# Gate and up projections by Strassen's seven products, operands in two hand-managed SBUF arenas

## The chip, the core and the metric

The kernel runs on one core of a Trainium2 chip, as one launch. The metric is the device time of an execution in microseconds; the medians compared here are of several executions. A profiled execution gives the trace from which all rows below are taken; its span is the time from its first to its last recorded work.

## What is computed

One decoder block over 512 tokens of width 2048, all in float32. Two token mixers run in parallel (latent attention with 16 heads, and a gMLP-style spatial gating unit), their outputs are merged by sigmoid gates, projected and added to the input, and a SwiGLU feed-forward of width 5632 and a last RMSNorm follow:

```
a = rms_norm(h, norm_mix_g);  z = a @ w_in            # q_lat, kv_lat, k_pe, uv, gate_logits
y_attn = mla(q_lat, kv_lat, k_pe, ...) @ w_o_attn;    y_sgu = sgu(uv, ...) @ w_o_sgu
merged = gates[0] * y_attn + gates[1] * y_sgu
h = h + merged @ w_out
f = rms_norm(h, norm_ffn_g)
h = h + (silu(f @ w_gate_ffn) * (f @ w_up_ffn)) @ w_down_ffn      # w_gate, w_up: 2048 x 5632
return rms_norm(h, norm_final_g)
```

## The kernel before

Every large product is made with float32 operands that are split into a high part (`fp32r`, rounded by a ScalarE cast) and a low part (source minus high, one VectorE subtraction). A product is then three matmuls into one PSUM bank: low x high, high x high, high x low (`mm3`, lines 98 to 101). A matmul takes 128 x 128 weights and up to 512 moving columns.

Weights lie in DRAM in blocks of 512 KB (128 partitions x 1024 floats). `chunk` (line 89) loads one block by SP's queue into a `raw` tile of the pool `wraw` (4 buffers), casts it on ScalarE (line 94) and subtracts on VectorE (line 95) into `whi` and `wlo` (3 buffers each). `gemm_fm` uses a block as the stationary operand (features come out on partitions, 512 tokens in the free dimension): 8 products, so 24 matmuls. `gemm_tm` uses it as the moving operand (tokens come out on partitions), 24 matmuls as well. Everything else is a 128 x 512 tile of one pool `big` (75 buffers), handed out by `T()`.

The stages follow each other in the text: latents, rotary tables, spatial gating unit, attention by pairs of heads, attention output, gates and merge, output projection with residual, feed-forward. Intermediate results stay in SBUF. In the feed-forward, `norm_in` transposes each quarter of `h` (line 546) and splits it into `fT` as soon as that quarter of `h` is there; the factor 1/rms of the tokens is applied after the matmuls, by a row `rfb` that is multiplied onto the PSUM banks (lines 582 and 584). `hidden(mp)` makes 256 of the 5632 hidden features: four blocks of w_gate and four of w_up alternate, 192 matmuls of 512 columns; there are 22 of them, 4224 matmuls. After 6 or 8 tiles of hidden features `down` multiplies them with their rows of w_down and adds into `h`. The last block of `down` and the final norm run by token blocks.

The order on each engine is set by a scheduler that arranges the written instructions by its own estimates; on the chip each engine then works through its list in that order, and semaphores make it wait for its operands.

Of the kernel before, what the change touches and what calls it, by code (L numbers as in the profile page):

```python
# [9 lines left out]
F32 = mybir.dt.float32  # L10
# [31 lines left out]
BIG, WR, WS = 75, 4, 3  # L42
FMAX = float(np.finfo(np.float32).max)


@with_exitstack
def tile_block(ctx: ExitStack, tc, a):
# [9 lines left out]
    def T(dt=F32):  # L57
        return big.tile([P, 512], dt, tag="t", name="t")
# [4 lines left out]
    def small(n, tag):  # L63
        return sml.tile([P, n], F32, tag="s%d" % n, name=tag)

# [8 lines left out]
    ones = con[:, C_ONE:C_ONE + P]  # L74

    def split(src, gain=None, n=512):
        hi, lo = T(F32R), T(F32R)
        if n < 512:
            hi, lo, src = hi[:, :n], lo[:, :n], src[:, :n]
        if gain is None:  # L80
            nc.scalar.copy(hi, src)  # L81
            nc.vector.tensor_tensor(out=lo, in0=src, in1=hi.bitcast(F32), op=ALU.subtract)  # L82
        else:
            nc.scalar.activation(hi, src, AF.Copy, scale=gain)
            nc.vector.scalar_tensor_tensor(
                out=lo, in0=src, scalar=gain, in1=hi.bitcast(F32), op0=ALU.mult, op1=ALU.subtract)
        return hi, lo

    def chunk(src, n=1024):
        raw = wraw.tile([P, 1024], F32, tag="raw", name="raw")  # L90
        hi = wsp.tile([P, 1024], F32R, tag="whi", name="whi")
        lo = wsp.tile([P, 1024], F32R, tag="wlo", name="wlo")
# [3 lines left out]
        return hi[:, :n], lo[:, :n]  # L96
# [6 lines left out]
    def gemm_fm(banks, w, kq, xs, first, last):  # L103
        """banks[m] += w[k-quad, 256 columns]^T @ xs (feature-major)."""
        hi, lo = chunk(w)
        hi = hi.rearrange("p (k m) -> p k m", k=4)
        lo = lo.rearrange("p (k m) -> p k m", k=4)
        for m, ps in enumerate(banks):
            ms = slice(m * P, (m + 1) * P)
            for k in range(4):  # L110
                xh, xl = xs[kq * 4 + k]
                mm3(ps, hi[:, k, ms], lo[:, k, ms], xh, xl, first and k == 0, last and k == 3)

    def gemm_tm(banks, w, kp, xs, first, last):
        """banks[tb] += xs^T @ w[k-pair, 512 columns] (token-major)."""
        hi, lo = chunk(w)
        for tb, ps in enumerate(banks):
            ts = slice(tb * P, (tb + 1) * P)
            for k in range(2):
                xh, xl = xs[kp * 2 + k]  # L120
                ws = slice(k * 512, (k + 1) * 512)
                mm3(ps, xh[:, ts], xl[:, ts], hi[:, ws], lo[:, ws], first and k == 0, last and k == 1)

    def rsqrt(ss, width, n, tag):
        """1/sqrt(ss/width + eps) with one Newton step behind the table's square root."""
# [13 lines left out]
    def sumsq(parts, n, tag):  # L139
        """Sum of squares along the free axis of each list of tiles: [P, n]."""  # L140
        k = len(parts[0])
        acc = small(n * k, tag + "a")
        for i, tiles in enumerate(parts):
            for j, t in enumerate(tiles):
                junk = T()
# [7 lines left out]
    def row_bcast(r, tag):  # L153
        """[P, NB] per-token columns -> the same values along the free axis on each partition."""
        ps = PS()
        for tb in range(NB):
            dg = T()[:, :P]
            nc.vector.tensor_scalar(out=dg, in0=ident, scalar1=r[:, tb:tb + 1], scalar2=None, op0=ALU.mult)
            nc.tensor.matmul(ps[:, tb * P:(tb + 1) * P], ones, dg, start=True, stop=True)  # L159
        out = T()  # L160
# [4 lines left out]
    def load_x(xs, k):  # L165
        """Tiles 2k and 2k + 1 of the gained x, feature-major."""
        raw = wraw.tile([P, 1024], F32, tag="raw", name="raw")
        nc.sync.dma_start(raw, a["xT"][k])
        for j in range(2):
            v = V_MIX + k * 2 + j  # L170
            xs.append(split(raw[:, j * 512:(j + 1) * 512], vec[:, v:v + 1]))

# [3 lines left out]
    def x_stats(tb):  # L176
        for c in range(4):
            t, junk = T(), T()
            nc.sync.dma_start(t, a["x"][tb * P:(tb + 1) * P, c * 512:(c + 1) * 512])
            nc.scalar.activation(junk, t, AF.Square, accum_out=xacc[:, tb * 4 + c:tb * 4 + c + 1])  # L180

# [34 lines left out]
    posi = big.tile([P, 512], I32, tag="t", name="posi")  # L216
# [11 lines left out]
    sinT = cst.tile([P, 512], F32, name="sinT")  # L228
    cosT = cst.tile([P, 512], F32, name="cosT")
# [3 lines left out]
    nc.scalar.activation(cosT, ang, AF.Sin)  # L233

    def rope(src):
        """The rotated [2 x 64 rope features, tokens]."""
        rot, out = T(), T()
# [4 lines left out]
        nc.vector.tensor_tensor(out=out, in0=out, in1=rot, op=ALU.add)  # L242
        return out

# [1 line left out]
    raw = wraw.tile([P, 1024], F32, tag="raw", name="raw")  # L246
    nc.sync.dma_start(raw, a["w_kpe"])
    kps = PS()
    for half in range(2):
        wk = wsp.tile([P, 1024], F32R, tag=("whi", "wlo")[half], name="wk").rearrange("p (k o m) -> p k o m", k=8, o=2)  # L250
# [7 lines left out]
    rxb = row_bcast(rx, "rxb")  # L258
    kpe = T()
    for own, other in ((slice(0, 64), slice(64, 128)), (slice(64, 128), slice(0, 64))):  # L260
        nc.scalar.copy(kpe[own], kps[other])
        nc.vector.tensor_tensor(out=kpe[own], in0=kps[own], in1=kpe[own], op=ALU.add)
    nc.vector.tensor_tensor(out=kpe, in0=kpe, in1=rxb, op=ALU.mult)
# [6 lines left out]
    vv = [[None, None] for _ in range(NB)]  # L270
    for g in range(2):
        banks = [PS() for _ in range(NB)]
        for kp in range(8):
            gemm_tm(banks, a["w_v"][g, kp], kp, aT, kp == 0, kp == 7)
        for tb, ps in enumerate(banks):
            t = T()
            nc.scalar.activation(t, ps, AF.Gelu_apprx_tanh, scale=rx[:, tb:tb + 1])
            vv[tb][g] = t
    rv = rsqrt(sumsq(vv, NB, "sv"), SGUW, NB, "rv")
    for tb in range(NB):  # L280
        for g in range(2):
            nc.vector.tensor_scalar(out=vv[tb][g], in0=vv[tb][g], scalar1=rv[:, tb:tb + 1], scalar2=None,
                                    op0=ALU.mult)

    kpe = rope(kpe)
    kph = cst.tile([P, 512], F32R, name="kph")
    kpl = cst.tile([P, 512], F32R, name="kpl")
    nc.scalar.copy(kph, kpe)
    nc.vector.tensor_tensor(out=kpl, in0=kpe, in1=kph.bitcast(F32), op=ALU.subtract)

    ut = []
    for mp in range(4):
        banks = [PS(), PS()]
        for kq in range(4):
            gemm_fm(banks, a["w_u"][mp, kq], kq, aT, kq == 0, kq == 3)
        for ps in banks:
            t = T()
            nc.vector.tensor_tensor(out=t, in0=ps, in1=rxb, op=ALU.mult)
# [430 lines left out]
```

## Time and profile before

| | us |
|---|---|
| median of 3 runs | 2789.36 |
| lowest and highest | 2789.19, 2790.16 |
| profiled execution, span | 2788.1 |
| TensorE busy in it | 2769.5 |
| VectorE, ScalarE busy in it | 1125.1, 843.1 |
| bytes read from HBM | 273.92 MB, 100 GB/s over the span |

The medians lie 1.3 us above the profiled span. Busy times of TensorE are sums of records that overlap: a 512-column matmul is recorded with 0.39 us and its successor starts 0.23 us later, so spacing, not duration, tells what a matmul costs in a stream. The same holds, by some 0.09 us, for records of VectorE that follow each other without a wait. "PEld" is TensorE's weight load, which runs beside the matmuls.

### The profile page before, as it was taken

How to read it: one execution, taken by the hardware profiler on the slowest of the kernel's cores; microseconds unless marked ns; L12 is line 12 of the kernel's file. 1: busy time of each engine (PE TensorE's matmuls, PEld its weight loads, DVE VectorE, ACT ScalarE, POOL GpSimd, SP SyncE). 2: the span in 40 equal slices, each digit the busy share in tenths (PEclk: the TensorE clock that was granted, in tenths of full speed). 3: DMA queues.
4: the chain of work that ended last, by engine and by line, in shares of the span. 5: the costliest groups of instructions: out<-in, count | busy, mean ns of one | idle time of the engine just before them, and what ended most of it. 6: DMA issues, size and time to landing. Idle time of an engine off the chain costs nothing.

```text
span 2788.1 us, 30320 instructions
## 1 busy us (share of the span) xinstructions
PE 2769.5 (99%) x12712; PEld 2312.9 (83%) x12712; DVE 1125.1 (40%) x1470; ACT 843.1 (30%) x1195; POOL 15.4 (1%) x31
## 2 busy tenths in 40 slices
PE   8999999999999999999999999999999999999998
PEld 7888988888888888888888888888888888888887
DVE  3433867742433333532433333333333333343345
ACT  5332565621322222332322122212221222222223
POOL 0000000000000000100000000000000000000000
PEclk9999999999999999999999999999999999999999
DMA  7323211222423322432223323323222322223232
GB/s 249 101 91 96 79 53 54 70 90 97 154 97 98 98 98 93 153 102 91 91 98 98 99 92 98 98 98 99 94 96 98 98 99 96 94 98 98 99 121 91
DMA packets 79752, 280.07 MB, mean 100 GB/s; under 512 B 9152, under 2 KB 9152, under 8 KB 79616
## 3 DMA queue, kind: packets, MB, share of 16 engines
q1 hardware_dynamic: 76176, 268.99, 29.4%
q0 software_dynamic: 2000, 6.56, 0.7%
q10 hardware_dynamic: 1440, 2.60, 0.3%
q8 instruction: 99, 1.62, 0.2%
q14 instruction: 37, 0.30, 0.0%
HBM read 273.92 MB, written 4.19 MB: 100 GB/s over the span
## 4 chain that ended last, share of the span: by engine, by line
PE 99%; DVE 0%; DMA 0%; ACT 0%; issue 0%; SPq 0%
PE b L99 32%; PE b L101 32%; PE b L100 32%; PE b L446 1%; PE b L425 0%; PE b L426 0%; PE b L546 0%; PE b L341 0%; DMA raw<-in_w_lat 0%; PE b L328 0%; ACT whi L94 0%; DVE wlo L95 0%; PE b L159 0%; DVE t L266 0%; DVE t L82 0%
## 5 line engine op out<-in xcount | busy, mean ns | idle before, releaser
L95 DVE TENSOR_TENSOR wlo<-raw,whi 128x1024 fp32r<-128x1024 f32 (+1 forms) x480 | 583.3, 1216 | 1416.0 <-ACT whi L94 1415.7
L99 PE MATMUL b<-t,wlo 128*128 128x512 f32 x2592 | 1008.8, 389 | 0.0
L101 PE MATMUL b<-t,whi 128*128 128x512 f32 x2592 | 1008.5, 389 | 0.0
L100 PE MATMUL b<-t,whi 128*128 128x512 f32 x2592 | 1008.5, 389 | 0.0
L94 ACT CAST whi<-raw 128x1024 fp32r<-128x1024 f32 (+1 forms) x480 | 501.6, 1046 | 1588.7 <-PE b L101 977.2
L99 PEld LDWEIGHTS b<-t,wlo 128*128 128x128 f32 x2592 | 486.6, 188 | 101.5 <-DVE wlo L95 0.2
L101 PEld LDWEIGHTS b<-t,whi 128*128 128x128 f32 x2592 | 486.6, 188 | 100.9
L100 PEld LDWEIGHTS b<-t,whi 128*128 128x128 f32 x2592 | 486.6, 188 | 100.7
L99 PE MATMUL b<-whi,t 128*128 128x512 f32 (+1 forms) x1280 | 486.3, 380 | 7.9 <-ACT whi L94 7.9
L101 PE MATMUL b<-wlo,t 128*128 128x512 f32 (+1 forms) x1280 | 485.5, 379 | 0.0
L100 PE MATMUL b<-whi,t 128*128 128x512 f32 (+1 forms) x1280 | 485.3, 379 | 0.0
L99 PEld LDWEIGHTS b<-whi,t 128*128 128x128 f32 x1280 | 241.4, 189 | 52.7 <-ACT whi L94 7.9
L101 PEld LDWEIGHTS b<-wlo,t 128*128 128x128 f32 x1280 | 241.3, 188 | 45.8 <-DVE wlo L95 0.8
L100 PEld LDWEIGHTS b<-whi,t 128*128 128x128 f32 x1280 | 241.4, 189 | 45.1
L596 DVE TENSOR_TENSOR t<-b,t 128x512 f32<-128x512 f32 x96 | 66.1, 689 | 32.4 <-PE b L101 31.9
L81 ACT CAST t<-t 128x512 fp32r<-128x512 f32 x84 | 49.3, 623 | 98.4 <-DVE t L585 96.4
L82 DVE TENSOR_TENSOR t<-t 128x512 fp32r<-128x512 f32 x84 | 55.7, 689 | 32.9 <-ACT t L81 32.9
L99 PE MATMUL b<-t 128*128 128x512 f32 (+2 forms) x192 | 66.3, 346 | 1.2 <-DVE t L82 1.2
L100 PE MATMUL b<-t 128*128 128x512 f32 (+2 forms) x192 | 66.3, 345 | 0.0
L101 PE MATMUL b<-t 128*128 128x512 f32 (+2 forms) x192 | 66.2, 345 | 0.0
L82 DVE TENSOR_TENSOR t<-b,t 128x512 fp32r<-128x512 f32 (+1 forms) x96 | 58.2, 662 | 15.6 <-ACT t L81 15.3
L81 ACT CAST t<-b 128x512 fp32r<-128x512 f32 (+1 forms) x96 | 49.1, 586 | 30.0 <-PE b L101 29.8
(187 smaller groups left out, 950.3 us busy)
## 6 DMA issues: line engine op xcount, KB each, us to landing
raw<-in_w_gate SPq DMA_DIRECT2D x88, 512.0 KB, 3.3
raw<-in_w_up SPq DMA_DIRECT2D x88, 512.0 KB, 3.3
raw<-in_w_down SPq DMA_DIRECT2D x88, 512.0 KB, 3.3
raw<-in_w_g SPq DMA_DIRECT2D x64, 512.0 KB, 3.3
raw<-in_w_oattn SPq DMA_DIRECT2D x32, 512.0 KB, 3.3
raw<-in_w_out SPq DMA_DIRECT2D x32, 512.0 KB, 3.3
raw<-in_xT SPq DMA_DIRECT2D x16, 512.0 KB, 4.6
raw<-in_w_lat SPq DMA_DIRECT2D x16, 512.0 KB, 4.5
```

The lines of the kernel that those rows point to most:

```text
L81: nc.scalar.copy(hi, src)
L82: nc.vector.tensor_tensor(out=lo, in0=src, in1=hi.bitcast(F32), op=ALU.subtract)
L94: nc.scalar.copy(hi[:, :n], raw[:, :n])
L95: nc.vector.tensor_tensor(out=lo[:, :n], in0=raw[:, :n], in1=hi[:, :n].bitcast(F32), op=ALU.subtract)
L99: nc.tensor.matmul(ps, sl, mh, start=first, stop=False)
L100: nc.tensor.matmul(ps, sh, mh, start=False, stop=False)
L101: nc.tensor.matmul(ps, sh, ml, start=False, stop=last)
L446: nc.tensor.transpose(out=pb[b][:, c:c + P], in_=src, identity=ident)
L596: nc.vector.tensor_tensor(out=h[tb][c], in0=ps, in1=h[tb][c], op=ALU.add)
```

## The change

**Gate and up.** A matrix product of 2 x 2 blocks can be made with seven block products instead of eight (the form used is Winograd's, with 15 sums). `forms_x` makes seven forms of each pair of feature tiles: of the blocks b11 and b12 (even feature tile, first and last 256 tokens) and b21 and b22 (odd tile). A form is a 512-wide tile that holds its high part in the first 256 columns and its low part in the last. `pair_gemm` (44 calls: 22 times w_gate, 22 times w_up) loads the four blocks of 256 output columns into one `raw` tile of 4096 floats per partition, sees them as quarters a11, a21, a12 and a22 that each run through all four blocks, makes the sums s1 to s4 on VectorE (s3, s2 and s4 overwrite a21, a11 and a12), and splits each of the seven operands (`form_w`). `product` issues, for each of 8 steps, one matmul of the high weights against the whole 512-wide form (high and low part side by side) and one of the low weights against the 256 high columns. Three PSUM banks collect the seven products, and VectorE and ScalarE add them up into the output.

**Normalisation.** `h` is multiplied by 1/rms before it is transposed, after all of W_out, and the transposed tiles become forms; no factor is applied after the matmuls.

**Memory.** The pools `big`, `wraw` and `wsp` are replaced by two tiles, `ar` (144 units of 256 floats per partition, high and low parts) and `af` (52 units, float tiles), from which an `Arena` hands out spans when the program is written: `get(n)` looks at starts at multiples of n (16 for 16) and takes the span whose latest release is oldest; spans of under 4 units avoid the first 32 units of `af`. `drop` gives spans back. The 112 units of the forms leave 32 units of `ar` for split weights: four pairs of high and low part.

**Spills.** For that space, gelu outputs (`utd`), the mixed tiles (`sgd`), attention heads (`ogd`), both branches' outputs (`ysd`, `ytd`), `h` (`hd`) and the hidden features (`hidd`) are written to DRAM and read back, mostly by POOL's queue. All hidden features are made before `down` starts; `down` runs over groups of 8 tiles, the next group being loaded and split while one is multiplied.

```diff
+class Arena:
...
+    def get(self, n):
+        best = None
+        for i in range(0, len(self.free_at) - n + 1, n if n < 16 else 16):
+            span = self.free_at[i:i + n]
+            if None not in span:
+                cost = (n < 4 and i < self.keep, max(span), -i)
+                if best is None or cost < best[0]:
+                    best = cost, i
...
+    def put(self, *aps):
+        for ap in aps:
+            _, i, n = self.held.pop(id(ap))
+            self.clock += 1
+            self.free_at[i:i + n] = [self.clock] * n
...
+    ar = Arena(cst.tile([P, NR * 256], F32R, name="ar"), NR)
+    af = Arena(cst.tile([P, NF * 256], F32, name="af"), NF, 32)
...
+        for src in (b11, b21, b22, t4, t1, t2, t3):
+            f = ar.get(2)
+            nc.scalar.copy(f[:, :256], src)
+            nc.vector.tensor_tensor(out=f[:, 256:], in0=src, in1=f[:, :256].bitcast(F32), op=ALU.subtract)
...
+    def form_w(src):
+        hi, lo = ar.get(4), ar.get(4)
+        hv, lv = (t.rearrange("p (k m) -> p k m", m=P) for t in (hi, lo))
+        nc.scalar.copy(hv, src)
+        nc.vector.tensor_tensor(out=lv, in0=src, in1=hv.bitcast(F32), op=ALU.subtract)
+        return hi, lo
+
+    def product(ps, w, i, first):
+
+        hi, lo = w
+        for kp in range(8):
+            ks = slice(kp * P, (kp + 1) * P)
+            x = fx[kp][i]
+            nc.tensor.matmul(ps, hi[:, ks], x, start=first and kp == 0, stop=False, skip_group_check=True)
+            nc.tensor.matmul(ps[:, :256], lo[:, ks], x[:, :256], start=False, stop=kp == 7, skip_group_check=True)
+        drop(w)
...
+    def pair_gemm(w):
+
+        raw = af.get(16)
         for kq in range(4):
-            gemm_fm(bg, a["w_gate"][mp, kq], kq, fT, kq == 0, kq == 3)
-            gemm_fm(bu, a["w_up"][mp, kq], kq, fT, kq == 0, kq == 3)
...
+            nc.sync.dma_start(raw[:, kq * 1024:(kq + 1) * 1024], w[kq])
+        quarters = raw.rearrange("p (k q m) -> p k q m", q=4, m=P)
+        a11, a21, a12, a22 = (quarters[:, :, q, :] for q in range(4))
+        ba, bb, bd = bank(), bank(), bank()
+        out = [T(), T()]
...
+        st = af.get(4)
+        s1 = st.rearrange("p (k m) -> p k m", m=P)
+        product(ba, form_w(a11), 0, True)
+        tt(s1, a21, a22, ALU.add)
+        s3 = tt(a21, a11, a21, ALU.subtract)
+        s2 = tt(a11, s1, a11, ALU.subtract)
+        u, u2, v = T(), T(), T()
+        nc.scalar.copy(u, ba)
+        product(bb, form_w(s2), 5, True)
+        tt(u2, bb, u, ALU.add)
+        product(bd, form_w(s3), 6, True)
+        product(bb, form_w(s1), 4, False)
+        tt(v, bb, u, ALU.add)
+        tt(v, bd, v, ALU.add)
+        both(c22, v)
+        drop(v)
+        product(ba, form_w(a12), 1, False)
+        nc.scalar.copy(c11, ba[:, 256:])
+        tt(c11, ba[:, :256], c11, ALU.add)
+        s4 = tt(a12, a12, s2, ALU.subtract)
+        product(bb, form_w(s4), 2, False)
+        tt(u, bb, u, ALU.add)
+        both(c12, u)
+        product(bd, form_w(a22), 3, False)
+        tt(u2, bd, u2, ALU.add)
+        both(c21, u2)
+        drop(u, u2)
+        drop(raw, st)
+        return out
```

What the scheduler made of it is seen at three places. First SP's queue, in the middle of gate and up; `DVE_49` is VectorE's semaphore, `DMAHW` those of earlier loads. Before:

```order
L93 DMA raw<-in_w_gate 128x1024 [waits DMAHW7_49,DVE_49]
L93 DMA raw<-in_w_up 128x1024 [waits DMAHW0_49,DVE_49]
L93 DMA raw<-in_w_gate 128x1024 [waits DMAHW1_49,DVE_49]
L93 DMA raw<-in_w_up 128x1024 [waits DMAHW2_49,DVE_49]
L93 DMA raw<-in_w_gate 128x1024 [waits DMAHW3_49,DVE_49]
```

and now:

```order
L725 DMA af<-in_w_gate 128x1024 [waits DMAHW7_49,DVE_49]
L725 DMA af<-in_w_gate 128x1024 [waits DMAHW0_49]
L725 DMA af<-in_w_gate 128x1024 [waits DMAHW1_49]
L725 DMA af<-in_w_gate 128x1024 [waits DMAHW2_49]
L725 DMA af<-in_w_up 128x1024 [waits DMAHW3_49,DVE_49]
L725 DMA af<-in_w_up 128x1024 [waits DMAHW4_49]
```

Each block waited for its own buffer before; now four blocks go together behind one wait for VectorE. Second ScalarE, over one pair (L701 is the cast of `form_w`, L738 the copy of `ba` to `u`, L748 that to c11, L764 Silu; `PE_49` and `Activation_49` are the semaphores of TensorE and ScalarE):

```order
L701 CAST ar<-af 128x1024 [waits DMAHW2_49,DMAHW7_49,DMAHW1_49,DMAHW0_49]
L701 CAST ar<-af 128x1024 [waits DVE_49,PE_49,Activation_49]
L764 ACTIVATE af<-af 128x512 [waits DVE_49]
L701 CAST ar<-af 128x1024 [waits DVE_49]
L701 CAST ar<-af 128x1024 [waits PE_49,Activation_49]
L738 COPY af<-b 128x512 [waits PE_49]
L701 CAST ar<-af 128x1024 [waits DVE_49]
L701 CAST ar<-af 128x1024 [waits DVE_49,PE_49,Activation_49]
L701 CAST ar<-af 128x1024 [waits PE_49]
L748 COPY af<-b 128x256 [waits PE_49]
```

Where one cast for each block stood before, seven casts and two copies stand now, and the copy of the first product has two casts that wait for TensorE around it. Third VectorE at the start of a pair (L702 is the low part of `form_w`; L107 are the sums, 128x1024 being s1 and 128x8x128 s3, s2 and s4):

```order
L107 TENSOR_TENSOR af<-af 128x1024 [waits DMAHW5_49,DMAHW6_49,DMAHW4_49,DMAHW3_49]
L107 TENSOR_TENSOR af<-b,af 128x512 [waits PE_49]
L702 TENSOR_TENSOR ar<-af,ar 128x1024 [waits Activation_49]
L107 TENSOR_TENSOR af<-af 128x256 [waits DVE_49]
L107 TENSOR_TENSOR af<-af 128x8x128
L107 TENSOR_TENSOR af<-af 128x512 [waits DVE_49]
L107 TENSOR_TENSOR af<-af 128x8x128 [waits DVE_49]
L702 TENSOR_TENSOR ar<-af,ar 128x1024 [waits Activation_49]
```

The low part of a11 stands third, behind s1 and behind an addition that reads the last bank of the pair before.

## Rows read from the trace of the kernel before

**Rows 1.** Page, part 1: busy us of each engine, share of span, instructions

```profile
PE 2769.5 (99%) x12712; PEld 2312.9 (83%) x12712; DVE 1125.1 (40%) x1470; ACT 843.1 (30%) x1195; POOL 15.4 (1%) x31
```

**Rows 2.** Waits: ScalarE's longest; us in total, times, longest

```profile
ACT whi L94 <- PE b L101: 977.2, 285, 4.7
```

**Rows 3.** Windows: stretch, length, busy (instructions) by engine, clock, DMA share, GB/s

```profile
1440.00:1700.00 260.00, 260.00 (x1148) 215.29 (x1148) 90.26 (x96) 60.21 (x64) 0.00 (x0) 1.00 0.30 96
```

**Rows 4.** Timeline, TensorE, values projection: start us, duration us, what

```profile
334.41 0.28 PE L101 MATMUL b<-wlo,t 128*128 128x256 f32 x1
...
339.80 0.28 PE L101 MATMUL b<-wlo,t 128*128 128x256 f32 x1
```

**Rows 5.** Groups by shape, VectorE: count, busy us, mean ns, idle before

```profile
L95 DVE TENSOR_TENSOR wlo<-raw,whi 128x1024 fp32r<-128x1024 f32 x464 | 568.1, 1225 | 1396.7 <-ACT whi L94 1396.4
L427 DVE CUSTOM_DVE_ANT_0 t<-b,con 128x256 f32<-128x256 f32 x16 | 6.8, 423 | 8.2 <-PE b L426 7.5
L253 DVE TENSOR_TENSOR wk<-raw,wk 128x512 fp32r<-128x512 f32 x2 | 1.3, 688 | 3.8 <-ACT wk L252 3.8
```

**Rows 6.** Timeline, VectorE, operations back to back in the feed-forward

```profile
1386.68 1.22 DVE L95 TENSOR_TENSOR wlo<-raw,whi 128x1024 fp32r<-128x1024 f32 x1
1387.81 0.68 DVE L582 TENSOR_TENSOR t<-b,t 128x512 f32<-128x512 f32 x1
1388.41 0.68 DVE L584 TENSOR_TENSOR t<-b,t 128x512 f32<-128x512 f32 x1
```

**Rows 7.** Groups by shape, ScalarE

```profile
L94 ACT CAST whi<-raw 128x1024 fp32r<-128x1024 f32 x464 | 488.9, 1054 | 1569.4 <-PE b L101 968.0 <-PE b L100 498.3 <-issue 98.4
L81 ACT CAST t<-b 128x512 fp32r<-128x512 f32 x80 | 45.3, 600 | 30.0 <-PE b L101 29.8
```

**Rows 8.** DMA issues: KB each, median us from issue to landing

```profile
raw<-in_w_gate SPq DMA_DIRECT2D x88, 512.0 KB, 3.3
t<-in_x POOLq DMA_DIRECT2D x16, 256.0 KB, 4.4
```

**Rows 9.** Timeline, SP's queue, start of the kernel: four loads of 512 KB

```profile
0.81 0.39 SPq L168 DMA_DIRECT2D raw<-in_xT  x1
...
2.19 0.47 SPq L93 DMA_DIRECT2D raw<-in_w_lat  x1
```

**Rows 10.** Windows at the start of the kernel, columns as in rows 3

```profile
3.00:4.00 1.00, 0.00 (x0) 0.00 (x0) 0.00 (x0) 0.00 (x0) 0.00 (x0) 1.00 1.03 402
8.00:9.00 1.00, 1.00 (x2) 0.42 (x2) 1.00 (x1) 0.61 (x1) 0.00 (x0) 1.00 1.04 426
```

**Rows 11.** Chain in order of time, and DMA issues, first 5 us

```profile
1.25 5.55 DMA raw<-in_w_lat
...
raw<-in_w_lat SPq DMA_DIRECT2D x2, 512.0 KB, 6.5
con<-in_consts ACTq DMA_DIRECT2D x1, 448.5 KB, 6.2
```

**Rows 12.** Timeline, TensorE: transposes of one quarter of `h`

```profile
1203.53 2.04 PE L546 MATMUL b<-con,t 128*128 128x128 f32 x16
```

**Rows 13.** Timeline, VectorE: the small operations of 1/rms, first and last

```profile
100.77 0.16 DVE L127 TENSOR_SCALAR rlv<-lacc 128x8 f32<-128x8 f32 x1
...
102.05 0.17 DVE L136 TENSOR_TENSOR rlo<-rlr,rlt 128x8 f32<-128x8 f32 x1
```

**Rows 14.** Timeline, TensorE, its first matmuls

```profile
7.92 0.80 PE L99 MATMUL b<-whi,t 128*128 128x512 f32 x1 [7.92 <-ACT whi L94]
...
13.56 0.40 PE L99 MATMUL b<-whi,t 128*128 128x512 f32 x1
```

**Rows 15.** Timeline, TensorE, after a wait late in attention

```profile
557.60 0.50 PE L99 MATMUL b<-t 128*128 128x512 f32 x1 [1.22 <-DVE t L82]
...
558.18 0.40 PE L101 MATMUL b<-t 128*128 128x512 f32 x1
```

**Rows 16.** Groups, TensorE's weight loads

```profile
L100 PEld LDWEIGHTS b<-whi,t 128*128 128x128 f32 x1280 | 241.4, 189 | 45.1
```

More of the change, by code (lines that the diff above doesn't have):

```diff
@@ L171, in load_x @@
             xs.append(split(raw[:, j * 512:(j + 1) * 512], vec[:, v:v + 1]))
+        drop(raw)
     aT = []
@@ L242, in rope @@
         nc.vector.tensor_tensor(out=out, in0=out, in1=rot, op=ALU.add)
+        drop(rot)
         return out
-    raw = wraw.tile([P, 1024], F32, tag="raw", name="raw")
+    raw = af.get(4)
     nc.sync.dma_start(raw, a["w_kpe"])
@@ new lines, in tile_block @@
+    qnT, kvT = latT
+    rv = rsqrt(sumsq(vv, NB, "sv"), SGUW, NB, "rv")
+    for tb in range(NB):
+        for g in range(2):
+            nc.vector.tensor_scalar(out=vv[tb][g], in0=vv[tb][g], scalar1=rv[:, tb:tb + 1], scalar2=None,
+                                    op0=ALU.mult)
+    rope(kp0, kpe)
+    kph = ar.get(2)
+    kpl = ar.get(2)
+    nc.scalar.copy(kph, kpe)
+    nc.vector.tensor_tensor(out=kpl, in0=kpe, in1=kph.bitcast(F32), op=ALU.subtract)
+    drop(kp0, kpe)
+    utd = drm.tile([G, P, 512], F32, name="utd")
@@ L377, in q_rope @@
             out.append(t)
+        drop(pe)
         return out
@@ L435, in scores @@
             out.append(dst)
-        return out
+        drop(qs, qp, ks)
+        return out, tiles
     def transposed(pr):
@@ L455, in values, with load @@
             mm3(ps[:, q0:], vh[:, o:o + P], vl[:, o:o + P], ph, pl, j == 0, j == NB - 1)
+        return ps
+    ogd = drm.tile([KD, P, 512], F32, name="ogd")
+    ytd = drm.tile([KD, P, 512], F32, name="ytd")
+    ysd = drm.tile([KD, P, 512], F32, name="ysd")
+    def load(src):
         t = T()
-        nc.vector.tensor_copy(t, ps)
+        nc.gpsimd.dma_start(t, src)
         return t
@@ L493, in tile_block, with gate @@
         for kq in range(4):
-            if mp == 0 and kq >= 2:
-                oT[kq * 4:kq * 4 + 4] = [split(t) for t in oT[kq * 4:kq * 4 + 4]]
             gemm_fm(banks, a["w_oattn"][mp, kq], kq, oT, kq == 0, kq == 3)
-        for ps in banks:
+            if mp == 7:
+                drop(oT[kq * 4:kq * 4 + 4])
+        for i, ps in enumerate(banks):
             t = T()
             nc.vector.tensor_copy(t, ps)
-            mrg.append(t)
+            nc.gpsimd.dma_start(ytd[mp * 2 + i], t)
+            drop(t)
     aT = []
-    def gate(w, b, mp, load=False):
+    mrg = []
+    def gate(w, b, mp, load=False, last=False):
         banks = [PS(), PS()]
@@ new lines, in tile_block, with hidden @@
+    for mp in range(DFF // 256):
+        gate = pair_gemm(a["w_gate"][mp])
+        for t in gate:
+            nc.scalar.activation(t, t, AF.Silu)
+        for i, t in enumerate(pair_gemm(a["w_up"][mp])):
+            tt(t, t, gate[i], ALU.mult)
+            nc.gpsimd.dma_start(hidd[mp * 2 + i], t)
+            drop(t, gate[i])
+    drop(fx)
+    for tb in range(NB):
+        for c in range(4):
+            h[tb][c] = load(hd[tb, :, c * 512:(c + 1) * 512])
+    def hidden(k0, n):
+        return [move(load(hidd[k])) for k in range(k0, k0 + n)]
```

382 lines of the change are left out of this document (217 added, 165 removed).

## Prediction, made before the run

> **What bounds the kernel now.** I read the busy totals first: TensorE is busy for 2769.5 of the 2788.1 us span [rows 1]. The waits come next: ScalarE's casts, on which VectorE's subtractions follow, stand idle for TensorE for 977 us [rows 2], so before the change any work on these two is free until it makes TensorE wait. TensorE's rate comes last. In a stretch of pure 512-column matmuls, 260 us hold 1148 of them, 0.2265 us each [rows 3]; that is the number to use, not the 0.39 us of one record, since records overlap. For 256 columns the values projection shows 45 steps between 334.41 and 339.80, 0.120 us each [rows 4].
>
> **The gain on TensorE.** Gate and up took 4224 matmuls of 512 columns: 4224 x 0.2265 = 957 us. Now each of the 44 calls of `pair_gemm` (a "pair" below: one weight matrix, 256 output columns) issues 7 products of 8 steps, a 512 and a 256 each: 56 x (0.2265 + 0.120) = 19.4 us, 854 us for all 44. Alternating widths are not in the trace; the two pure rows bound them. If TensorE never waited, 103 us would be gone.
> [...]
>
> **VectorE and ScalarE as engines.** Per pair VectorE has 11 operations of 1024 elements, 5 or 6 of 512 and 4 of 256. Records last 1.225, 0.688 and about 0.42 us [rows 5], but back to back a 1024 takes 1.13 and a 512 0.60 [rows 6]; I take 0.35 for a 256. Sum 12.4 + 3.3 + 1.4 = 17.1 us, under 19.4. The new operands are strided by quarters; the strided key weights of L253 take 688 ns for 512, like contiguous ones [rows 5], so no surcharge. ScalarE has 7 casts of 1024, two copies and a Silu, some 9 us [rows 7]. Neither is the bound by its sum. The question is the order in which they wait.
>
> **The load is not double-buffered.** `raw` takes 16 units at 0, 16 or 32 of the float arena. 32 nearly always holds some T tile. `st` (4 units) may lie anywhere and lands in 0, the half that was free longest; `drop(raw, st)` then gives `st` the later clock, so half 0 counts as younger than half 16, and the next `raw` takes half 16 again, the one just released. Working the allocator through, 42 of 44 pairs load into the same half. The SP rows show the result: the first of each four loads waits for VectorE, that is for the low part of a22, the last reader of `raw`. ScalarE's first cast then waits for all four landings, because every quarter runs through all four blocks.
> The landing of 2 MB: a lone 512 KB takes 3.3 us [rows 8]. At the start of the kernel four such loads are issued from 0.81 to 2.19 us [rows 9] and the engines move 402 to 426 GB/s [rows 10]. So 3.3 + 3 x 0.524 MB / 0.41 = 7.1 us. From the other side: the two w_lat loads took 5.55 and, with their median at 6.5, 7.45 us, so the last landed at 9.64, 8.8 us after the first issue, with a further 448 KB among them worth 1.1 us [rows 11]: 7.7. I take 7.4, between 6.5 (first bytes earlier) and 8.8.
> [...]
>
> **One pair, step by step**, from the landing as zero, with 0.05 us for a semaphore. ScalarE casts a11 high, 0.05 to 1.10; TensorE's first matmul at 1.15. The second needs a11 low, which stands on VectorE behind s1 (1.14) and an addition of the pair before (0.60): ready at 3.02. TensorE idles 1.7. The first product issues until 5.6. Then the order puts one matmul of a12's product, into the same bank, ahead of s2's; it needs the a12 cast (0.95 to the next) and the copy of the bank to u (0.6): 7.4, TensorE idles 1.8. Then s2's cast: 8.4, idles 0.75. The products of s2 and s3 end at 14.1, which frees the weight slot for a22: cast and low part until 16.5. Four loads: 16.5 + 7.4 = **23.9 us**.
> TensorE's own loop is as long: 19.4 plus the waits. If the load came early, a11's low part would still stand behind the addition that waits for the previous pair's last product: 0.2 + 0.6 + 1.23 against one matmul, a wait of 1.85; 19.4 + 1.85 + 1.8 + 0.75 = 23.8. So a faster load saves next to nothing and a slower one costs in full: 23.5 to 25.3 us. 44 x 23.9 = 1052, against 957: **+95 us** (+77 to +156).
>
> **The rest.**
> - Entry to the gate: the normalisation was applied after the matmuls and its transposes ran inside TensorE's stream, 64 of them, 2.04 us per 16 [rows 12], 8 us in all. Now everything waits for the last W_out column: add, square, statistics (0.69 + 0.82 + 1.28 table + 1.45 for the small VectorE chain [rows 13], some 4 us), then 8 scalings and 88 operations of 256 elements on VectorE (0.40 and 0.33 back to back: 32 us) against 8 scalings, 16 copies and 56 casts of 256 on ScalarE (0.64, 0.60 and, carried on below the two widths of [rows 7], some 0.34: 34 us), which alternate, then the first a11 forms, 3 us. 43 minus 8: **+35** (28 to 45).
> - Into attention: gelu tiles go to DRAM and back; w_sgu's load (256 KB by POOL, as in_x 4.4 us [rows 8]) now waits for the T slots of the last gelu tiles, and the first query weights for slots that the mixing holds: one round trip of 4.4 + 0.6 + transposes and one of slot release + 3.3 + 2.2, some 7 and 15 us: **+22** (5 to 35), since nothing lies beside them on TensorE.
> - Into down: the first w_down blocks wait for float and weight slots that the last pair holds: release + 3.3 + 1.05 + 1.23 behind 16 splits: **+12** (5 to 25). `hidd` is read early and lies beside it.
> - The other spills (ysd, ytd, ogd, the x reload) are POOL loads and stores beside 150 us stretches of matmuls: 0. That cover is W_osgu's 7 groups for the attention output; without it one load and split, 6 us.
> [...]
>
> **Rivals.**
> - *TensorE always finds its operands* (faster): a pair at 19.4 us is -103, with +77 for the rest 2762 us. It decides below (957 - 77) / 44 = 20.0 us a pair, waits under 0.6 us. The SP order and the three chained ScalarE steps speak against it. 2%; another 2% for the space between it and 2900, half of it within the bound of no change.
> - *The load is slower*: the stores of `hidd` or strided reads slow it to 10 us or more. The load loop is then 26.5 us, 44 x 2.6 = +114, some 3075 us. For it: spills share the engines. Against: before, they moved 96 GB/s [rows 3] and now little more. 8%.
> - [...] 5%. [...]
> - *The 256-column matmul is bound by its weight load*, 189 ns a record [rows 16]: +0.068 x 56 = 3.8 us a pair on TensorE's loop, 44 x 3.7 = +163, 3125 us. The 0.120 spacing, each with its own weights, speaks against it. 3%.
>
> **How the numbers follow.** Span 2788.1 + 95 + 35 + 22 + 12 + 8 = 2960; the median stands 1.3 us above the span: **2961 us**. This case has 80%, from 2900 (all low ends but one: 77 + 28 + 5 + 5 = 115) to 3060 (156 + 45 + 35 + 25 + 15 = 276, short of all high ends at once). The rivals lie outside; 2 in 10 are left out. A measurement of this kernel tells 0.2% (5.6 us) from no change. Faster 0.02, within it 0.01, slower 0.97.
>
> **What the next profile would show.** The four loads of a pair issued about 16 us after the landing before, and landing 7 to 8 us later; a cast at L701 waiting for them; TensorE at L712 waiting for VectorE and at L711 for ScalarE, some 1.8 us each, and busy about 81% over 1050 us; a gap of some 40 us ahead of the first L711. I am wrong if loads start while the pair before still multiplies its first products, if a pair takes under 22 us, or if the spacing at L711 and L712 sums to more than 0.36 us.

## The result, and the profile after

The changed kernel takes 3078.46 us (median of 4 runs, 3068.57 to 3092.47) against 2789.28: 1.104 times the time before, 95% interval 1.1011 to 1.1069. The forecast was slower, 2961 us, from 2900 to 3060; the time lies 117 us above it and 18 us above the range. The profiled run is the slowest of the four (span 3090.7, 302.6 more than before).

The page of the changed kernel: busy us by engine; the granted clock in 40 slices; groups (count, busy, mean ns, idle before); DMA issues (KB, us to landing).

```profile
PE 2832.8 (92%) x13408; PEld 2359.0 (76%) x13408; DVE 1652.8 (53%) x2161; ACT 1035.3 (33%) x1480; POOL 144.7 (5%) x271
PEclk9999999999999999998898999988898988999999
L711 PE MATMUL b<-ar 128*128 128x512 f32 x2464 | 968.9, 431 | 122.2 <-ACT af L738 62.2
L712 PE MATMUL b<-ar 128*128 128x256 f32 x2464 | 723.8, 300 | 59.1 <-DVE ar L702 59.0
af<-in_w_gate SPq DMA_DIRECT2D x88, 512.0 KB, 4.7
```

Against [rows 1] TensorE went from 99% to 92% busy, and in the slices from 18 on the clock is no longer full everywhere. A 512-column record takes 431 ns on average, against the 0.39 us that the prediction named for one of before. The waits that the prediction named are here: a11's low part at L712 (59.0 us), the a12 matmul at L711 (62.2 us behind L738), and s2's cast in the rest of L711's idle time, all of it behind L701; that rest also holds the entry and, in some pairs, a wait for a11's cast. A load of 512 KB now lands after 4.7 us as one of four, 3.3 before [rows 8].

TensorE's records around the other terms of the sum: last matmul or wait, and its releaser.

```profile
290.68 1.97 PE L395 MATMUL b<-con,af 128*128 128x128 f32 x8 [6.01 <-POOL af L391]
313.23 0.77 PE L148 MATMUL b<-ar 128*128 128x512 f32 x1 [12.46 <-DVE ar L143]
680.53 0.79 PE L148 MATMUL b<-ar 128*128 128x512 f32 x1 [6.33 <-ACT ar L125]
1369.15 0.39 PE L150 MATMUL b<-ar 128*128 128x512 f32 x1
1414.15 0.79 PE L711 MATMUL b<-ar 128*128 128x512 f32 x1 [14.09 <-ACT ar L701]
2584.99 0.28 PE L712 MATMUL b<-ar 128*128 128x256 f32 x1
2600.12 0.79 PE L148 MATMUL b<-ar 128*128 128x512 f32 x1 [14.85 <-ACT ar L142]
```

| part | forecast, us over before | measured |
|---|---|---|
| gate and up | 44 x 23.9 = 1052, +95 | 1414.15 to 2585.1: 1171, **+214** |
| entry to the gate | 43 - 8 = +35 | 1369.38 to 1414.15: 44.8 - 8 = +37 |
| into attention | +22 | 6.0 + 12.5 = +18 |
| attention output | 0 (6 without cover) | +6 |
| into down | +12 | +15 |
| clock outside the pairs, remainder | +8 | 302.6 - 290 = +13 |

All but the first line are within 7 us. The 119 us by which gate and up missed are 2.7 us in each of the 44 pairs. Four pairs, from the first issue of one load to the next (window: length, busy with instructions by engine, granted clock, DMA share, GB/s):

```profile
1560.10:1584.12 24.02, 20.49 (x112) 16.87 (x111) 19.03 (x22) 8.10 (x9) 1.08 (x2) 1.00 0.30 110
1720.84:1746.41 25.57, 21.84 (x112) 18.10 (x111) 19.12 (x22) 8.10 (x9) 1.08 (x2) 0.93 0.28 103
1477.07:1504.48 27.41, 23.87 (x116) 19.62 (x115) 17.82 (x20) 9.25 (x11) 0.00 (x0) 0.88 0.21 77
2146.31:2176.76 30.45, 25.38 (x112) 20.64 (x111) 19.20 (x22) 8.09 (x9) 1.08 (x2) 0.78 0.23 87
```

At the full clock a pair takes 24.02 us, the forecast's 23.9. But of the 38 pairs whose four loads are issued together, one load after the other, only 4 kept it, with 24.0 to 24.6 us; the others ran 25 to 31 us. Multiplying length by what the clock lacks gives 1.8, 3.3 and 6.7 us for the last three rows; they are 1.6, 3.4 and 6.4 us longer than the first. Over the whole stretch:

```profile
1452.78:2585.22 1132.44, 968.17 (x4755) 797.93 (x4754) 781.14 (x893) 367.44 (x426) 33.58 (x63) 0.90 0.25 92
```

10% of 1132 us is 113 us, nearly all of the miss. Late loads have a share: 8 of the 38 landed 8.7 to 9.4 us after their first issue, the others after 7.3 to 8.0, at most some 12 us in all by my estimate (8 times 1.5). TensorE's records show where it falls, here in a pair with 0.94:

```profile
1911.71 0.51 PE L711 MATMUL b<-ar 128*128 128x512 f32 x1 [1.53 <-ACT ar L701]
1913.66 0.39 PE L712 MATMUL b<-ar 128*128 128x256 f32 x1 [1.45 <-DVE ar L702]
...
1918.04 0.49 PE L711 MATMUL b<-ar 128*128 128x512 f32 x1 [1.55 <-ACT af L738]
1918.99 1.22 PE L711 MATMUL b<-ar 128*128 128x512 f32 x2 [0.45 <-ACT ar L701]
...
1920.22 0.63 PE L711 MATMUL b<-ar 128*128 128x512 f32 x1
1920.65 0.41 PE L712 MATMUL b<-ar 128*128 128x256 f32 x1
1920.86 0.63 PE L711 MATMUL b<-ar 128*128 128x512 f32 x1
```

Four waits of 1.53, 1.45, 1.55 and 0.45 us stand close together; behind the last, 512 columns take 0.43 us and 256 take 0.21 (1920.22 to 1920.65 to 1920.86) at a granted clock of 0.50, where the full clock has 0.2265 and 0.120 [rows 3], [rows 4]. The first of the four is not needed for it: 16 pairs without a wait of over 0.25 us for a11's cast fell too, and three of the four pairs at the full clock have the same waits of 1.4, 1.55 and 0.45 us as some of these.

### The profile page after: what moved, and what is told of

Its sections match the earlier page's. It is cut to its first block, busy times and chain, and to the rows that moved or that the text cites. A ratio compares the mean times of both kernels' runs of the same rounds, so it can differ in the third digit from the quotient of the medians.

```text
span 3090.7 us, 33517 instructions
## 1 busy us (share of the span) xinstructions
PE 2832.8 (92%) x13408; PEld 2359.0 (76%) x13408; DVE 1652.8 (53%) x2161; ACT 1035.3 (33%) x1480; POOL 144.7 (5%) x271
## 4 chain that ended last, share of the span: by engine, by line
PE 62%; DMA 11%; DVE 7%; ACT 6%; issue 3%; SPq 2%; POOL 0%; DVEq 0%; ACTq 0%; POOLq 0%
PE b L150 15%; PE b L148 15%; PE b L149 15%; PE b L711 10%; PE b L712 5%; DMA af<-in_w_gate 4%; DMA af<-in_w_up 4%; ACT ar L701 4%; DVE ar L702 3%; DVE af L107 3%; SPq L725 2%; ACT af L738 1%; PE b L522 1%; DMA af<-ogd 1%; PE b L501 0%
## 5 line engine op out<-in xcount | busy, mean ns | idle before, releaser
L711 PE MATMUL b<-ar 128*128 128x512 f32 x2464 | 968.9, 431 | 122.2 <-ACT af L738 62.2
L148 PE MATMUL b<-ar 128*128 128x512 f32 (+1 forms) x2656 | 1017.5, 383 | 43.7 <-ACT ar L142 22.9
L150 PE MATMUL b<-ar 128*128 128x512 f32 (+1 forms) x2656 | 1015.7, 382 | 0.2
L149 PE MATMUL b<-ar 128*128 128x512 f32 (+1 forms) x2656 | 1015.6, 382 | 0.0
L712 PE MATMUL b<-ar 128*128 128x256 f32 x2464 | 723.8, 300 | 59.1 <-DVE ar L702 59.0
L711 PEld LDWEIGHTS b<-ar 128*128 128x128 f32 x2464 | 502.2, 205 | 276.4 <-ACT ar L701 87.4
L143 DVE TENSOR_TENSOR ar<-af,ar 128x1024 fp32r<-128x1024 f32 (+1 forms) x304 | 364.8, 1209 | 604.3 <-ACT ar L142 542.5
L148 PEld LDWEIGHTS b<-ar 128*128 128x128 f32 x2656 | 501.8, 189 | 140.2 <-ACT ar L142 23.2
L150 PEld LDWEIGHTS b<-ar 128*128 128x128 f32 x2656 | 501.6, 189 | 98.2 <-DVE ar L143 1.5
L149 PEld LDWEIGHTS b<-ar 128*128 128x128 f32 x2656 | 502.1, 189 | 95.4
L712 PEld LDWEIGHTS b<-ar 128*128 128x128 f32 x2464 | 510.3, 207 | 80.9 <-DVE ar L702 73.6
L142 ACT CAST ar<-af 128x1024 fp32r<-128x1024 f32 (+1 forms) x304 | 312.7, 1040 | 736.2 <-PE b L149 310.3
L701 ACT CAST ar<-af 128x1024 fp32r<-128x1024 f32 x308 | 320.7, 1048 | 497.9 <-PE b L711 304.9
L702 DVE TENSOR_TENSOR ar<-af,ar 128x1024 fp32r<-128x1024 f32 x308 | 368.4, 1219 | 43.4 <-ACT ar L701 40.5
L107 DVE TENSOR_TENSOR af<-af 128x1024 f32<-128x1024 f32 (+2 forms) x440 | 343.0, 801 | 57.2 <-DMA af<-in_w_up 26.0
L107 DVE TENSOR_TENSOR af<-b,af 128x512 f32<-128x512 f32 (+1 forms) x264 | 170.4, 645 | 275.9 <-PE b L712 227.8
L748 ACT COPY af<-b 128x256 f32<-128x256 f32 x44 | 16.4, 372 | 194.4 <-PE b L712 194.4
L767 POOL DMA_DIRECT2D hidd<-af x44 | 23.8, 541 | 1115.1 <-DVE af L107 1114.7
```

The source lines that it names most:

```text
L107: nc.vector.tensor_tensor(out=out, in0=in0, in1=in1, op=op)
L148: nc.tensor.matmul(ps, sl, mh, start=first, stop=False)
L149: nc.tensor.matmul(ps, sh, mh, start=False, stop=False)
L150: nc.tensor.matmul(ps, sh, ml, start=False, stop=last)
L701: nc.scalar.copy(hv, src)
L702: nc.vector.tensor_tensor(out=lv, in0=src, in1=hv.bitcast(F32), op=ALU.subtract)
```

## The experiments

**The load.** Is TensorE's own loop as long as the load's, as the prediction said? First, s1 gets a place of its own, so that the halves alternate.

```diff
+    st = af.get(4, 32)      # held for the whole stage, above the halves (get now takes a first place)
     def pair_gemm(w):
-        st = af.get(4)
...
-        drop(raw, st)
+        drop(raw)
```

> The changed kernel with one thing different: s1 gets a place of its own above the two halves, so that loads alternate between the halves and each load can start a whole pair earlier. The order of the instructions follows (the lone a12 matmul ahead of s2's product is gone). By the step of the prediction (TensorE's own loop is as long as the load's, a faster load saves next to nothing): 23.8 us a pair, 3060 to 3080 us. Theory now (the waits at the head of the pair bring TensorE's clock down, and it is these that the early load takes away): no cast at L701 waits for the loads, PE waits under 2 us a pair, granted clock at least 0.98, 20 to 22 us a pair, 2800 to 2890 us.

Measured: 2786.3 us (median of 10), 0.9975 of the kernel before (0.9958 to 0.9993); 292 us are gone. TensorE's groups in the stage, then windows of two pairs:

```profile
L711 PE MATMUL b<-ar 128*128 128x512 f32 x2464 | 875.1, 400 | 4.7 <-ACT af L739 1.8 <-ACT ar L701 1.4 <-DVE af L107 0.9
L712 PE MATMUL b<-ar 128*128 128x256 f32 x2464 | 694.2, 282 | 2.4 <-DVE ar L702 2.4
```

```profile
1878.07:1897.74 19.67, 19.67 (x114) 17.05 (x113) 18.56 (x22) 8.12 (x9) 1.08 (x2) 1.00 0.35 135
1897.74:1917.66 19.92, 19.92 (x115) 17.31 (x114) 17.54 (x20) 9.19 (x12) 0.00 (x0) 1.00 0.28 105
```

7 us of waits in the whole stage, 19.8 us a pair, clock 1.00. The pair does not stay at 23.8 us, as the step had it, and the expectation was too cautious. The code differs by where one tile lies, but the built order differs more: the lone a12 matmul is gone, and a11's low part stands ahead of the addition that reads the previous pair's last bank. So the early load came with another order, and this run does not tell the two apart.

Second, the same half, but half the bytes.

```diff
-            nc.sync.dma_start(raw[:, kq * 1024:(kq + 1) * 1024], w[kq])
+            nc.sync.dma_start(raw[:, kq * 1024:kq * 1024 + 512], w[kq][:, :512])
+        nc.gpsimd.memset(raw.rearrange("p (b n) -> p b n", b=4)[:, :, 512:], 0.01)
```

> The changed kernel, but each of the four loads of a pair brings half of its bytes (the other half of the block is set to a constant by GpSimd, so the products are not those of the reference). The order of the instructions stays. Theory (TensorE's own waits set the pair as much as the load does, and the clock is what is missing from the forecast): the loads land about 2 us earlier, the wait ahead of the first matmul of the pair (1.0 to 1.5 us) goes, the other three waits and the slow stretches stay: at most 1.5 us a pair, 3010 to 3075 us, granted clock below 0.97. Rival (the load loop is the bound, and its 9 us landings are what the forecast missed): 2 us or more a pair and the pairs without a slow stretch fall below 22.5 us, 2990 us or less.

Measured: 2962.76 us (median of 4). Windows of two pairs at the full clock and one below it:

```profile
1895.84:1917.85 22.01, 19.90 (x114) 17.11 (x113) 17.64 (x20) 9.02 (x11) 1.81 (x1) 1.00 0.15 48
2304.01:2326.54 22.53, 20.52 (x115) 17.39 (x114) 18.67 (x22) 8.01 (x9) 2.89 (x3) 1.00 0.21 71
2326.54:2350.22 23.68, 21.09 (x111) 17.87 (x110) 17.55 (x20) 9.00 (x11) 1.81 (x1) 0.93 0.14 46
```

The load becomes some 2 us shorter, and so does the pair at the same clock: 24.0 to 22.0 and 22.5. These are the rival's numbers. But the order did not stay: the addition with the previous pair's last product now stands behind a11's low part, which waits 0 to 0.5 us instead of 1.44, and in many pairs of w_up no a12 matmul waits ahead of s2's product any more. So the pair lost a wait of TensorE together with load time, and that the load alone was the bound is not shown. In the changed kernel both loops end together: in the pair of 24.02 us the load has landed at 1567.64, and TensorE, busy with the pair before until about 1568.5, starts at 1568.74. The other part of the 2.6 us a pair is clock: 0.93 over the stretch, not 0.90.

Third, the prediction priced the lone a12 matmul ahead of s2's product at 1.8 us. It is taken away by holding the matmuls in the order of the text.

```diff
+            a = nc.tensor.matmul(ps, hi[:, ks], x, ...)
+            tc.keep_in_program_order(a)     # the same for the matmul on lo
```

> The changed kernel with all loads still in one half, but TensorE's matmuls held in the order of the text, so that no matmul of a12's product stands ahead of s2's. Theory (the pair is the load's loop: a11 cast, products to the end of s3's, a22's cast and low part, load; each microsecond of wait ahead of s3's end costs in full): s3's product ends 1.9 us earlier, 22 to 23.6 us a pair at the full clock, 2950 to 3000 us. Rival (TensorE then waits for s2's cast and low part just as long): 3060 to 3090 us.

Measured: 3172.65 us, worse than both. TensorE's groups in the stage:

```profile
L711 PE MATMUL b<-ar 128*128 128x512 f32 x2464 | 993.1, 438 | 137.9 <-ACT ar L701 137.1
L713 PE MATMUL b<-ar 128*128 128x256 f32 x2464 | 759.8, 308 | 97.2 <-DVE ar L702 97.2
```

TensorE then waits for s2's cast itself, about 2.5 us in each pair, where the a12 matmul and s2's cast had waited 1.55 + 0.45, and for the low parts: 235 us in all, where the changed kernel has 122.2 + 59.1 = 181. A pair took 28.7 us on average at a granted clock of 0.87. The matmul out of turn had covered a wait, not made one.

**The clock.** What brings it down? Waits of known length are put into kernels that had none: ScalarE reads a bank in mid-accumulation, and the bank's next matmul waits for it, 0.85 us on average in the first of them. In all these runs the stage's matmuls are also held in the order of the text. Each run, like the one just told, is a single execution, and the version with alternating halves, from which four of them start, spreads from 2768 to 2789 us by itself; the waits and the clock of a trace say more than 20 us of its time. The expectations price a fall of the clock at 2 to 2.9 us, an estimate; its upper end is that of [rows 14], where TensorE's first 12 matmuls issue in 5.64 us (7.92 to 13.56) and 12 x 0.2265 would be 2.72. First the kernel before, waits in groups of three and evenly spread.

```diff
                 mm3(ps, hi[:, k, ms], lo[:, k, ms], xh, xl, first and k == 0, last and k == 3)
+                if (m, k) in stops:
+                    nc.scalar.copy(probe, ps)
```

> The kernel before, its gate and up matmuls unchanged in kind and order (512 columns, three each), but ScalarE reads a bank in mid-accumulation and the bank's next matmul has to wait for it: 132 such waits of an estimated 1.2 us, in 44 groups of three (0.7 and 2.7 us of matmuls between them), one group in about 22 us, as the pairs of the changed kernel have them. [...] Rival (the clock falls for the alternating widths or the traffic of the changed kernel, not for waits): 2947 us, granted clock 1.00.

> As the run with the waits together: the same 132 waits in the same stage of the kernel before, but evenly apart, 7 us of matmuls between one and the next. Theory (it takes several waits near each other): 2947 us, granted clock 1.00. [...]

2941.34 and 2934.54 us, granted clock 0.999 in both. TensorE's group with the waits, of the first and of the second:

```profile
L103 PE MATMUL b<-t,wlo 128*128 128x512 f32 x2592 | 1024.0, 395 | 112.8 <-ACT probe L119 112.8
L103 PE MATMUL b<-t,wlo 128*128 128x512 f32 x2592 | 1024.8, 395 | 104.8 <-ACT probe L119 104.7
```

112.8 / 132 = 0.85 us a wait by the record, (2941.3 - 2789.6) / 132 = 1.15 in time, 0.30 more than the record. The spread waits give the same: 104.7 us by the record, 144.9 in time, 0.30 for each of 132. Behind three such waits in a group the clock did not fall. So longer ones, and the same two lengths in the version with alternating halves, whose pairs have 512 and 256 columns in turn:

> As the run with the waits together (the kernel before, 512 columns only, 44 groups of three waits), but ScalarE reads the bank twice, so that each wait is 0.58 us longer: about 1.43 us by the record and 1.73 us in time, as long as the waits in the pairs of the changed kernel. Three theories for the clock that fell there. A, the length of the waits in a group decides: 2789 + 132 x 1.73 = 3018 us for the waits, and 44 x 2 to 2.9 for the clock on top, 3105 to 3145 us, granted clock about 0.95. B, the alternating widths decide: 3018 us, clock 1.00. C, neither, it is the late loads and their traffic: 3018 us, clock 1.00.

> The version with loads in alternating halves (no waits of its own in a pair, 512 and 256 columns in turn), with three waits of one bank read each in every pair, 0.85 us by the record and 1.15 in time: after the second step of the first product, the second and the fourth step of the second. A (length decides): 2786 + 132 x 1.15 = 2938 us, granted clock as there, 0.98 or more. B (the alternating widths make a group of short waits enough): 2938 + 88 to 128, 3025 to 3065 us, granted clock about 0.94. C: 2938 us.

> As the run before, with two bank reads to a wait: the alternating widths and waits as long as in the changed kernel, while the loads come early. A and B: 2786 + 132 x 1.73 = 3014 us and 88 to 128 for the clock, 3100 to 3140 us, granted clock about 0.94. C (late loads and their traffic bring the clock down): 3014 us and no slow stretches.

| run | mean wait, longest that recurs | time | waits at record + 0.30 | left over, a group | groups or pairs with a lower clock |
|---|---|---|---|---|---|
| 512 only, short (above) | 0.85, 1.5 | 2941.3 | +152 | 0 | 0 of 44 |
| 512 only, long | 1.48, 2.1 | 3066.8 | +235 | 43, 1.0 us | 18 of 44 |
| alternating, short | 1.10, 1.9 | 3006.0 | +185 | 35, 0.8 us | 22 of 41 |
| alternating, long | 1.73, 2.5 | 3166.0 | +268 | 112, 2.5 us | 41 of 41 |

The 0 of the first row is so by construction, since the 0.30 comes from that run; the granted clock shows it. The last run has slow pairs like the changed kernel's although its loads come early; windows of two of them:

```profile
2142.74:2170.24 27.50, 22.76 (x114) 19.11 (x113) 18.76 (x22) 11.52 (x15) 1.08 (x2) 0.88 0.25 96
2225.67:2255.90 30.23, 24.47 (x114) 20.26 (x113) 17.91 (x20) 12.56 (x17) 0.00 (x0) 0.83 0.19 70
```

So theory C (late loads) is out as the cause: with early loads and the same traffic the clock was full without these waits (1.00 in the windows of the alternating halves) and low with them (0.88 and 0.83 here). A is right in direction, but between 512-column matmuls fewer than half of the groups fell, and its price there was twice too high. For B the third run says little, since its waits were uneven: in nearly all of its pairs without a fall they were 0.86, 1.35 and 0.73 us, in nearly all with one 1.90, 0.7 to 1.2 and 0.73, the first behind a Silu. Windows of one of each:

```profile
2148.31:2171.50 23.19, 20.25 (x114) 17.03 (x113) 18.67 (x22) 9.78 (x12) 1.08 (x2) 1.00 0.31 114
2171.50:2198.57 27.07, 23.33 (x114) 19.52 (x113) 17.82 (x20) 10.81 (x14) 0.00 (x0) 0.87 0.22 78
```

Two more runs keep the waits short, or put all into one.

> As the run with alternating widths and three short waits in a pair, but the waits stand in the fourth and fifth product (second step of s1's, second and fourth of a12's), where ScalarE is not held up by the Silu; in the other run one wait in every second pair had grown to 1.9 us, and only those pairs fell. A (the length of the single waits decides): if none is above 1.4 us, granted clock in gate and up at least 0.99 and 2786 + 132 x (measured wait + 0.30), some 2940 to 2970 us. B (with alternating widths short waits are enough): granted clock there 0.96 or less and 35 us or more on top of that sum.

> The version with loads in alternating halves with a single wait in each pair, three bank reads long, an estimated 2.3 us by the record (0.85 and twice 0.58 and 0.25 as in the other runs) and 2.6 in time, in s1's product. If the length of the longest wait decides, the clock falls in most pairs: 2786 + 44 x 2.6 = 2900 us and 1 to 2.5 us a pair on top, 2945 to 3010 us, granted clock there 0.90 to 0.96. If it takes several waits close together: 2900 us, clock there 0.99 or more.

A window over 900 us of gate and up of the run with later waits, and the same of the run with one wait (the clock is the third number from the end):

```profile
1500.00:2400.00 900.00, 800.39 (x4281) 669.57 (x4279) 697.47 (x804) 390.04 (x497) 20.61 (x38) 0.97 0.28 102
```

```profile
1500.00:2400.00 900.00, 825.46 (x4415) 708.18 (x4414) 717.20 (x829) 404.43 (x509) 25.87 (x48) 0.95 0.29 105
```

With later waits: 2958.22 us; 113.4 us of waits, 0.86 on average and none above 1.4, hence 2786 + 153 = 2939, and 19 us for the clock. Neither expectation came: A had 0.99 or more, B 0.96 or less. With one wait: 2927.63 us; it is 1.91 us (not 2.3), 2786 + 44 x 2.21 = 2883, and 44 us for the clock, 1.0 a pair. Within each run the pairs can be compared: 29 of 41 fell behind the single wait, and 16 of 41 with the later short ones; in both they are some 1.6 us longer than those of the same run that kept the clock. So the clock fell behind single waits too, in more pairs where waits were longer, and with short waits in this kernel but not between the 512-column matmuls of the kernel before. That it is the widths in which the two kernels differ there, and not their traffic or something else, is not shown; which pairs fall is not settled by these runs.

**The entries.** From the alternating halves on, the waits that remain are the entries. They were shortened in two goes; two of the changes of the first:

```diff
-    drop(fx, st)
+    for i in (0, 5, 6, 4, 1, 2, 3):      # forms in the order in which they die
+        drop([f[i] for f in fx])
...
-                    nc.tensor.transpose(out=ps[:, tb * P:(tb + 1) * P], in_=h[tb][c][:, k * P:(k + 1) * P], identity=ident)
+                    nc.tensor.matmul(ps[:, tb * P:(tb + 1) * P], h[tb][c][:, k * P:(k + 1) * P], dg[:, tb * P:(tb + 1) * P], start=True, stop=True)
```

> The version with loads in alternating halves (2786 us, no waits in gate and up but some 78 us of entries and exits that the kernel before does not have), with those shortened: the forms of x scaled by TensorE (a diagonal of the norm as the moving operand instead of 16 scalings) and their sums on GpSimd, down's first blocks into the forms that die first, the residual read when it is added, w_sgu and the first attention weights loaded ahead, half of the attention outputs read back earlier. Theory (these waits stand alone on TensorE's path, so what is cut there shows in full): entry 44 to 32 us, into down 12 to 3, into attention 20 to 6, attention output 5 to 0: 2786 - 40 = 2735 to 2755 us, faster than the kernel before by 1.2 to 2%. Rival (what is cut comes back as waits for slots, the two arenas being full): 2775 to 2790 us.

2761.86 us (median of 6), 0.9891 of before (0.9873 to 0.9909): between theory and rival. The entry gained little. The group of VectorE's 56 subtractions there, of the changed kernel and then of this one:

```profile
L670 DVE TENSOR_TENSOR ar<-af,ar 128x256 fp32r<-128x256 f32 x56 | 19.7, 416 | 0.0
```

```profile
L674 DVE TENSOR_TENSOR ar<-af,ar 128x256 fp32r<-128x256 f32 x56 | 31.7, 628 | 4.9 <-ACT ar L673 4.8
```

The mean of 628 ns mixes two kinds: those that ran beside a GpSimd sum mostly took 0.94 us, the others 0.41 as before. One of each, and the sum beside the first:

```profile
1360.62 0.94 DVE L674 TENSOR_TENSOR ar<-af,ar 128x256 fp32r<-128x256 f32 x1
1361.82 0.41 DVE L674 TENSOR_TENSOR ar<-af,ar 128x256 fp32r<-128x256 f32 x1
1360.37 0.91 POOL L669 TENSOR_TENSOR af<-af 128x256 f32<-128x256 f32 x1
```

Why the first takes longer is not shown.

> As the run with the entries shortened, with three things different: the sums of the forms are back on VectorE (there, subtractions of 256 columns on VectorE that ran beside GpSimd's sums took 0.5 to 0.6 us each instead of 0.345), the forms are made for two pairs of row blocks at a time in operations of twice 256 columns, and the w_sgu part stands ahead of the first gelu tiles, whose slot its second load waited for. Theory (VectorE's 28 subtractions and 16 sums at 0.6 us set the entry: 26 us and some 6 us of statistics and start): first gate matmul 34 to 38 us after the last W_out matmul and no second wait behind it, no wait at the w_sgu transposes, 2740 to 2753 us. Rival (the entry is set by the chain transposes, copies, sums, casts, and gains nothing): 2757 to 2765 us.

2743.99 us (median of 5), 0.9813 of before (0.979 to 0.9835): within the theory's range, 1.9% faster than before. No long wait is left into attention; the entry is still 41.6 us, from 1335.97 to

```profile
1377.55 0.80 PE L714 MATMUL b<-ar 128*128 128x512 f32 x1 [19.74 <-ACT ar L704]
```

(TensorE's timeline), not the 34 to 38 expected, since VectorE and ScalarE stood 3 us for the first gate load.

## Why the prediction was right and wrong

- *TensorE's rate.* Right. A step of 512 and 256 takes 0.3525 us (19.8 us a pair without a wait), 0.3465 expected; that is 0.4 us a pair. The bound by weight loads, which would make it 0.2265 + 0.189 = 0.4155 us, did not come.
- *The load is not double-buffered.* Right. In the pair of 24.02 us the cast waits until 1567.64, 7.5 us after the first issue at 1560.10 (7.4 expected), and the next load is issued at 1584.12, 16.5 us after that (16.5 expected). 8 of 38 loads took 8.7 to 9.4 us; why is open. The rival of a slower load (10 us, 3075 us) has the measured time as well, but not its mechanism: 30 of the 38 landed within 8.0 us.
- *One pair, step by step.* Right in places and sizes at the full clock: a11's low part 1.44 us (1.7), the a12 matmul 1.55 (1.8), s2's cast 0.46 (0.75); at the 0.30 us that a wait costs beyond its record, an estimate from the runs with known waits, the three come to 4.35 us, against 4.25. ScalarE's cast and TensorE's timeline of that pair:

```profile
1567.64 1.05 ACT L701 CAST ar<-af 128x1024 fp32r<-128x1024 f32 x1 [4.22 <-DMA af<-in_w_gate]
1570.68 0.38 PE L712 MATMUL b<-ar 128*128 128x256 f32 x1 [1.44 <-DVE ar L702]
1575.06 0.49 PE L711 MATMUL b<-ar 128*128 128x512 f32 x1 [1.55 <-ACT af L738]
1576.00 0.74 PE L711 MATMUL b<-ar 128*128 128x512 f32 x2 [0.46 <-ACT ar L701]
```

- *TensorE's own loop is as long, so a faster load saves next to nothing.* The first half is right for the order as built: in the pair of 24.02 us both loops end within 0.3 us of each other. The second half did not come: with half the load the pair at the full clock was 1.5 to 2 us shorter, with an early load 4.2. The step kept the order of the built program fixed while it changed the load that the order had been made for; in both runs the order moved with the load, so what a faster load would save in the old order stays untested. This did not move the forecast of the time.
- *The clock, +8 us in the sum.* **This is the step that failed.** It counted the falls behind the three long entries and none in the pairs. No run shows the 8 us as one figure; in its place the trace has a granted clock of 0.50 from 313.23 to 318.06, from 1414.15 to 1420.34 and from 2600.12 to 2604.96, behind the waits of 12.46, 14.09 and 14.85 us; what TensorE lost there is 2.3, 2.9 and 2.6 us by my estimate from its steps and the full rate. In the pairs the prediction had the clock full, and there it was 0.90 over gate and up. A fall in each pair had 5%, at 2.9 us a pair 44 x 2.9 = 128 us and 3090 us, and it is what came: about 2.6 us a pair and 3078 us. The price was right, the chance was not. The chance rested on one row, a single wait of 1.22 us behind which two matmuls of 512 columns still took 0.58 us together [rows 15], while the prediction's own ledger had three waits of up to 1.8 us within some 7 us; in the changed kernel the clock fell in 34 of the 38 pairs, with three or four waits of mostly 0.45 to 1.6 us in each.
- *The range.* Its upper end added nearly all high ends of the terms but left the clock in the pairs at zero, and so stopped at 3060. With 2.9 us a pair among the unknown costs it would have reached some 3190. None of the signs of being wrong that the text named came; none of them was on the clock.
- *The rest.* Entry, attention and down came within 4 us each, and the clock outside the pairs, with a remainder, took 13 us for 8; the attention output lost its cover and cost the 6 us that the text named as the price.
- *VectorE and ScalarE.* Not the bound: 19.03 and 8.10 us in a pair by records that overlap, against 17.1 and 9. With the load early VectorE is busy for some 18 of 19.8 us by such records and could be next.

## What to carry to other kernels

The waits that these matmul loops repeat had two prices, their length and in many pairs the clock (0.90 over gate and up of the changed kernel, 113 of 1132 us). Without a row of waits as long and as close as the forecast ones, the second belongs in the range at full size. Where a scheduler makes the order, a claim about "the same order with an earlier load" has to be read from the order built with that load. And an allocator that reuses the oldest slot can undo double buffering through one small tile: the place of four units of 52, with the order that came of it, made 292 us here.

## What the chip showed unexpectedly

- The granted clock fell with groups of waits of mostly 0.45 to 1.6 us (0.90 over gate and up of the changed kernel), and with a single 1.91 us wait in each pair (0.95), while three of 0.85 us between 512-column matmuls left it at 0.999 over the whole run.
- The same pair came out at 24.0, 25.6, 27.4 or 30.5 us, and pairs with the same waits fell or did not. The runs are wide too, 3068 to 3092 us, the longest with the lowest clock (0.949); the kernel before stays within 2 us.
- A wait of 0.85 us by the record cost 1.15 us in time, in two runs. About half of the difference, by my estimate, is the overlap of the records (0.39 us each, 0.23 from one to the next, so 0.16 of the 0.30), which a wait undoes; the rest is open.
- VectorE subtractions of 256 columns took 0.94 us instead of 0.41 beside GpSimd's sums.
